# State-space loop of a two-layer backbone: scan states in PSUM, all back rotations on VectorE, the last gelu product on GpSimd, modulation in sixteen pieces

## Chip, core, metric

The kernel runs on one core of a Trainium2 chip. The metric is the device time of one launch in microseconds (us). The engines are TensorE (PE in the profile), VectorE (DVE), ScalarE (ACT), GpSimd (POOL) and SyncE (SP), which issues the DMAs. Each works through its own queue in order and waits for the others by semaphores. Operands lie in SBUF or in PSUM, the eight banks into which TensorE writes.

## What is computed

A backbone of two layers over 1024 latent tokens and 256 context tokens, 1024 wide. Layer 0 mixes with differential attention, layer 1 with a bidirectional diagonal state-space layer (S5). The change lies in that state-space layer:

```python
def step(h, uc):
    bu = jnp.einsum('gpc,btgc->btgp', b_bar, uc.astype(jnp.complex64))
    a_cum, hs = lax.associative_scan(_linear_combine, (a, bu), axis=1)
    hs = hs + a_cum * h[:, None]
    y = jnp.real(jnp.einsum('gcp,btgp->btgc', c_mat, hs))
    return hs[:, -1], y
...
g = jax.nn.gelu(y.astype(h.dtype))
o1, o2 = jnp.split(jnp.einsum('btd,de->bte', g, w_glu), 2, axis=-1)
return o1 * jax.nn.sigmoid(o2)
```

There are 64 channel groups of 16 channels with 64 complex states each, a forward and a backward direction, and `a` is the same at every token. Beside it each layer needs six modulation vectors (shift, scale and gate, twice) from a product of one row with a 1024 x 6144 matrix, `ada_w`.

## The kernel before

The complex recurrence is made real by a rotation: the inputs are turned back by the angle that the state has gained up to their place, a real scan with the decay alone runs over the places, and its states are turned forward again. The method `s5` does it in `for n in range(19)`, which is written in software-pipelined form; for ScalarE, VectorE, GpSimd and TensorE the order of the code is the order of the queues (`with self.manual()`), only SyncE's is set by a scheduler. Step n takes the four channel groups 4n to 4n+3 for n up to 15; d is 0 forward and 1 backward. The parts, with the engine:

- `phase(n, d)` (GpSimd): the angles, an integer add of 128 x 640, into one of three buffers `phs`, which it may overwrite when the back rotations of three directions earlier have read it.
- `trig(n, d)` (ScalarE, four instructions): sine and cosine in place; `decay(n, d)` (ScalarE): the decay of each place into `rs`.
- `inputs(n, d)` (TensorE): the scan inputs into PSUM, two matrices j of 128 x 640 (`xbank`), four matmuls each. The profile shows each of these matmuls as two rows.
- `rotate(n, d)` (VectorE, two products from PSUM into `t1` and `t2`), and the sum `t1 + t2` (GpSimd).
- `scan(n, d)` (VectorE): the recurrence, 128 x 640, decay and input from SBUF.
- `back(n, d, j)` (four products of 128 x 512): states times cosine and sine into `cs`. Three are on VectorE; the last, backward, j = 1, is on GpSimd at the start of the next step.
- `outputs(n)` (TensorE, one step later): for each of four groups i five matmuls into bank 6 or 7.
- gelu of step m = n - 2: Square (ScalarE), `scalar_tensor_tensor` (VectorE), Tanh and `u + 1` (ScalarE), the product with y (VectorE) into `ggs`. The buffer `u` is one for all steps.
- `tr` (TensorE): four transposes into the bank whose output the gelu has read. At odd n they read the product of the same step, at even n older ones. `tr_out` (ScalarE, then VectorE in the next step): their result, split into a high and a low part.
- `modulation(i)`: one of eight halves of the layer's last four modulation vectors, 32 matmuls, a copy on ScalarE, a transpose, and two small VectorE instructions. Its weights (2 MB) are loaded over the part of `U` that the loop has consumed: `mods` holds for each half the step at whose end it is loaded and the step at whose end it is multiplied (20: behind the loop).

Behind the loop follow the last modulation halves, the last products of the GLU's first weight block (`first`), and the GLU itself.

Of the kernel before, what the change touches and what calls it, by code (L numbers as in the profile page):

```python
# [6 lines left out]
F32 = mybir.dt.float32  # L7
# [63 lines left out]
class Prog:  # L71
# [192 lines left out]
    def ada_half_load(self, ws, l, seg, half):  # L264
        c0 = 1024 * seg + 512 * half
        for kk, w in enumerate(ws):
            self.dma(w, self.I["ada_w"][l].rearrange("(k p) n -> p k n", p=128)[:, 2 * kk : 2 * kk + 2, c0 : c0 + 512])

    def ada_half_products(self, ws, l, seg, half, acc, t=None):
        nc = self.nc  # L270
        for k in range(8):
            for j in range(4):
                nc.tensor.matmul(acc[32 * j : 32 * j + 32], self.scT[:, 2 * k : 2 * k + 32],
                                 ws[k // 2][:, k % 2, 128 * j : 128 * j + 128], start=k == 0, stop=k == 7)
# [7 lines left out]
        nc.vector.scalar_tensor_tensor(m, acc.rearrange("p (j r) -> p r j", j=4)[:, 0:2], 1.0 if seg in (1, 4) else 0.0, m,  # L282
                                       ALU.add, ALU.add)
# [1569 lines left out]
    def s5(self):  # L1853
# [7 lines left out]
        u = self.fv(36, 4, 8, 16)  # L1861
# [6 lines left out]
        cs = [[(self.fv(x, 4, 128), self.fv(y, 4, 128)) for x, y in (((10, 32), (29.5, 34)), ((15, 22.5), (17.5, 22.5)))[d]]  # L1868
# [9 lines left out]
        mods = [(6, 8), (8, 10), (10, 12), (11, 13), (12, 14), (13, 15), (15, 20), (15, 20)]  # L1878
        halves = [[self.view(self.U, 16 * i + 4 * kk, (2, 512)) for kk in range(4)] for i in range(2)]
# [11 lines left out]
        def modulation(i, c):  # L1891
            self.ada_half_products(halves[i % 2 if i > 2 else 0], 1, 2 + i // 2, i % 2, self.PS[:, c : c + 128])
# [24 lines left out]
        def xbank(n, d, j):  # L1917
            b = 1024 * ((4 * n + 2 * d + j) % 3)
# [24 lines left out]

        def scan(n, d):
            t1, t2, r = (t.rearrange("p x n -> p (x n)") for t in (*ts[d][n % 2], rs[d][n % 2]))
            v.tensor_tensor_scan(t2, r, t1, 0.0, ALU.mult, ALU.add)

        def back(eng, n, d, j):
# [5 lines left out]
            eng.tensor_tensor(o, ts[d][n % 2][1][:, :, h], (Ps if j else Pc)[:, :, h], ALU.mult)  # L1954

        def outputs(n):
# [622 lines left out]
```

## Time and profile before

| | |
|---|---|
| median of 3 runs | 2849.98 us (2846.97 to 2850.45) |
| profiled execution | span 2849.8 us, 0.2 under the median; no other time of it is shown |
| TensorE, VectorE, ScalarE, GpSimd busy over the whole span | 96%, 71%, 48%, 36% |
| start of the forward scan of step 0, 2 and 15 | 1832.71, 1855.02, 2004.43 us |
| first matmul of `first(1, ...)`, behind the last modulation half | 2030.70 us |

A row of the timeline has the start from the span's beginning, the duration, engine, line and operation, the tiles (`FD` and `U` are SBUF, `PS` is PSUM, `H` and `W` are SBUF) and the number of equal instructions merged in it; a bracket at its end tells how long the engine stood idle before it and what ended that. Neighbouring instructions of one engine overlap by up to 0.1 us, so that what one costs is read from start to start. A row of the stretches has, for each engine, its busy time in the stretch, and at the end the clock granted to TensorE, the share of the DMA engines and the rate in GB/s. A row of the groups has the number of instructions, the busy time and the mean in ns of one, and the idle time before them.

### The profile page before, as it was taken

Reading aid. Unit: us, or ns where it says so; the run is one execution under the profiler, and the core shown is the slowest. Engines: PE = TensorE matmul, PEld = TensorE weight load, DVE = VectorE, ACT = ScalarE, POOL = GpSimd, SP = SyncE. Lnnn points to the kernel's source line nnn. Section 1 sums busy time; section 2 is a strip of 40 time slices with the busy share of each in tenths; the row PEclk is TensorE's granted clock in tenths of the full one; section 3 lists DMA queues with packets and bytes.
Section 4 is the critical chain, followed back from the end, with each engine's and each line's share of the span. In section 5 each row is a group of like instructions: output and inputs, shape, how many; then the busy total and the mean of one; then the engine's idle time right before and its main releaser. Section 6 shows DMA issues by size and latency. Waiting matters only on the chain.

```text
span 2849.8 us, 43385 instructions
## 1 busy us (share of the span) xinstructions
PE 2723.3 (96%) x15229; PEld 2283.1 (80%) x15229; DVE 2019.8 (71%) x2984; ACT 1369.5 (48%) x2583; POOL 1037.2 (36%) x901
## 2 busy tenths in 40 slices
PE   6999999999999999999999999789999999999999
PEld 4688888888877887778877878688887778888887
DVE  6357788888873667767698878799543597668466
ACT  3425555565653753333444445487444633344443
POOL 3314676766663600000030013688121143336414
PEclk9999999999999999999999999899999999999999
DMA  9955555655825359886799878579742144476544
GB/s 279 319 172 188 152 173 172 177 171 171 256 91 182 128 179 316 294 302 216 249 312 310 272 238 263 169 228 306 235 154 98 66 163 160 155 246 227 167 131 142
DMA packets 414823, 586.30 MB, mean 206 GB/s; under 512 B 41870, under 2 KB 260236, under 8 KB 411404
## 3 DMA queue, kind: packets, MB, share of 16 engines
q1 hardware_dynamic: 414604, 583.52, 63.5%
q8 instruction: 120, 1.97, 0.3%
q14 instruction: 99, 0.81, 0.1%
HBM read 396.38 MB, written 182.82 MB: 203 GB/s over the span
## 4 chain that ended last, share of the span: by engine, by line
PE 76%; DVE 9%; DMA 5%; issue 4%; POOL 3%; ACT 2%; SPq 1%; DVEq 0%; ACTq 0%; POOLq 0%
PE PS L132 21%; PE PS L134 20%; PE PS L133 20%; PE PS L581 4%; PE PS L627 2%; PE PS L1928 2%; PE PS L1963 2%; DMA FU<-in_mlp_w 1%; DMA Ta<-FU 1%; PE PS L202 1%; DVE R L138 1%; SPq L80 1%; DVE F L615 1%; ACT F L604 1%; DVE H L138 1%
## 5 line engine op out<-in xcount | busy, mean ns | idle before, releaser
L132 PE MATMUL PS<-H 128*128 128x512 f32 x1072 | 420.6, 393 | 2.7 <-ACT H L137 1.7
L134 PE MATMUL PS<-H 128*128 128x512 f32 x1072 | 417.5, 390 | 2.8 <-DVE H L138 1.5
L133 PE MATMUL PS<-H 128*128 128x512 f32 x1072 | 417.7, 390 | 0.0
L132 PE MATMUL PS<-H,R 128*128 128x512 f32 (+1 forms) x828 | 308.0, 374 | 4.3 <-ACT R L137 2.0
L133 PE MATMUL PS<-H,R 128*128 128x512 f32 (+1 forms) x828 | 298.6, 361 | 0.0
L134 PE MATMUL PS<-H,R 128*128 128x512 f32 (+1 forms) x828 | 298.0, 361 | 0.0
L132 PEld LDWEIGHTS PS<-H 128*128 128x128 f32 x1072 | 201.2, 188 | 50.5 <-issue 6.4
L134 PEld LDWEIGHTS PS<-H 128*128 128x128 f32 x1072 | 201.2, 188 | 46.1 <-DVE H L138 2.3
L133 PEld LDWEIGHTS PS<-H 128*128 128x128 f32 x1072 | 201.3, 188 | 40.6
L604 ACT ACTIVATE F<-F,stat 128x1280 f32<-128x1280 f32 x128 | 174.3, 1362 | 106.6 <-DVE F L594 106.5
L137 ACT ACTIVATE H<-U 128x640 fp32r<-128x640 f32 x216 | 131.9, 674 | 172.6 <-PE PS L133 138.3
L137 ACT ACTIVATE R<-W 128x512 fp32r<-128x512 f32 (+1 forms) x184 | 128.7, 707 | 174.1 <-PE PS L133 101.5
L132 PE MATMUL PS<-R,H 128*128 128x512 f32 x520 | 208.0, 401 | 3.3 <-ACT H L137 3.3
L134 PE MATMUL PS<-R,H 128*128 128x512 f32 x520 | 205.0, 396 | 1.8 <-DVE H L138 1.8
L133 PE MATMUL PS<-R,H 128*128 128x512 f32 x520 | 204.5, 394 | 0.0
L138 DVE TENSOR_TENSOR H<-U,H 128x640 fp32r<-128x640 f32 x216 | 165.1, 797 | 50.6 <-ACT H L137 49.6
L138 DVE TENSOR_TENSOR H<-W,H 128x512 fp32r<-128x512 f32 (+1 forms) x137 | 125.2, 924 | 102.8 <-ACT H L137 102.1
L594 DVE TENSOR_SCALAR_CACHE_REDUCE F<-PS 128x1280 f32<-128x1280 f32 x128 | 185.2, 1483 | 9.3 <-PE PS L581 9.1
L137 ACT ACTIVATE H<-W 128x512 fp32r<-128x512 f32 (+2 forms) x158 | 95.4, 613 | 188.7 <-PE PS L133 116.8
L132 PEld LDWEIGHTS PS<-H,R 128*128 128x128 f32 x828 | 157.6, 191 | 30.2 <-issue 4.1
L134 PEld LDWEIGHTS PS<-H,R 128*128 128x128 f32 x828 | 157.0, 190 | 25.2 <-issue 0.8
L641 POOL TENSOR_SCALAR R<-F 128x256 fp32r<-128x256 f32 (+1 forms) x128 | 126.5, 989 | 136.0 <-ACT F L640 122.4
(534 smaller groups left out, 6860.0 us busy)
## 6 DMA issues: line engine op xcount, KB each, us to landing
W<-in_mlp_w SPq DMA_DIRECT2D x176, 256.0 KB
U<-Aa SPq DMA_DIRECT2D x108, 320.0 KB
Aa<-FU SPq DMA_DIRECT2D x91, 320.0 KB
Ad<-F SPq DMA_DIRECT2D x112, 256.0 KB
W<-Ad SPq DMA_DIRECT2D x112, 256.0 KB
FU<-in_mlp_w SPq DMA_DIRECT2D x32, 512.0 KB
Ta<-FU SPq DMA_DIRECT2D x16, 1024.0 KB
U<-in_ada_w SPq DMA_DIRECT2D x32, 512.0 KB
```

Of the source, the lines that this page charges most:

```text
L132: mm(out, ah, bh, start=first, stop=False, **kw)
L133: mm(out, ah, bl, start=False, stop=False, **kw)
L134: mm(out, al, bh, start=False, stop=last, **kw)
L137: self.nc.scalar.activation(hi, src, AF.Copy)
L138: (lo_eng or self.nc.vector).tensor_tensor(lo, src, hi.bitcast(F32), ALU.subtract)
L581: mm(self.PS[:, 1280 * c + k0 : 1280 * c + k1], Q[:, c, r, qs], K[c][:, k0:k1], start=r == 0, stop=r == 1)
L594: ts(p[c], self.PS[:, 1280 * c : 1280 * c + 1280], 1.0, None, ALU.mult, ALU.min, accum_out=sm[:, c : c + 1])
L604: nc.scalar.activation(p[c], p[c], AF.Exp, bias=sm[:, c : c + 1], scale=-1.0, accum_out=sn[:, 0:1] if c else s0[:, u + 1 : u + 2])
L627: self.nc.tensor.transpose(tb[:, 128 * (kt - k0) : 128 * (kt - k0) + 128], w[:, 128 * kt : 128 * kt + 128], self.ident)
L641: nc.gpsimd.tensor_scalar(hi, t, 1.0, 0.0, ALU.mult, ALU.add)
L1928: mm(b[:, o : o + 160], X[:, d, i, 64 * j : 64 * j + 128], U[:, 4 * n + i, cols], start=True, stop=True)
L1963: mm(o, cs[d][n % 2][j][:, i], W[:, d, i], start=False, stop=d == 1 and j == 1)
```

## The change

Four things are changed in `s5`, with what they need around them.

1. `scan` writes its states to PSUM, columns 2048 to 2687, one buffer for both directions, instead of `t2`. For that `xbank` uses two areas (j = 0 and 1) for every step and direction instead of three in rotation.
2. All four back rotations are on VectorE and read the states from PSUM; the backward j = 1 outputs have two buffers.
3. Up to m = 14, ScalarE copies y to SBUF (`yc`) instead of making u + 1, and GpSimd makes u + 1 and the last product.
4. The modulation halves are cut into pieces: 16 of 1 MB with 16 matmuls each; the copy, the transpose and the small instructions follow a second piece. They start at step 3 and are multiplied one step after their load in most cases. The two small VectorE instructions go through PSUM where there is a gain.

Besides, the low part of `tr_out` stands ahead of the forward rotations, the first of the four output groups stands between the forward and the backward inputs on TensorE, and the backward `decay` moves behind `yc` on ScalarE. `FD` grows from 56 to 60 KB.

```diff
-    def ada_half_products(self, ws, l, seg, half, acc, t=None):
+    def ada_half_products(self, ws, l, seg, half, part, acc):
         nc = self.nc
-        for k in range(8):
+        for k in range(4 * part, 4 * part + 4):
             for j in range(4):
                 nc.tensor.matmul(acc[32 * j : 32 * j + 32], self.scT[:, 2 * k : 2 * k + 32],
-                                 ws[k // 2][:, k % 2, 128 * j : 128 * j + 128], start=k == 0, stop=k == 7)
-        if t is None:
-            t = self.adat[:, 0:128]
-            nc.scalar.activation(t, acc, AF.Copy)
-        else:
-            nc.vector.tensor_copy(t, acc)
+                                 ws[k // 2 % 2][:, k % 2, 128 * j : 128 * j + 128], start=k == 0, stop=k == 7)
+        if part == 0:
+            return
+        t = self.adat[:, 0:128]
+        nc.scalar.activation(t, acc, AF.Copy)
         nc.tensor.transpose(acc, t, self.ident)
         m = self.modc[:, l, seg, :, 4 * half : 4 * half + 4]
-        nc.vector.scalar_tensor_tensor(m, acc.rearrange("p (j r) -> p r j", j=4)[:, 0:2], 1.0 if seg in (1, 4) else 0.0, m,
-                                       ALU.add, ALU.add)
-        if seg in (1, 2, 4, 5):
+        a = acc.rearrange("p (j r) -> p r j", j=4)[:, 0:2]
+        gain = seg in (1, 2, 4, 5)
+        nc.vector.scalar_tensor_tensor(a if gain else m, a, 1.0 if seg in (1, 4) else 0.0, m, ALU.add, ALU.add)
+        if gain:
             g = self.ng[:, l, {1: 0, 2: 1, 4: 2, 5: 3}[seg], 4 * half : 4 * half + 4]
-            nc.vector.tensor_tensor(m, m, bcast(g, 1, 2), ALU.mult)
+            nc.vector.tensor_tensor(m, a, bcast(g, 1, 2), ALU.mult)
...
-        cs = [[(self.fv(x, 4, 128), self.fv(y, 4, 128)) for x, y in (((10, 32), (29.5, 34)), ((15, 22.5), (17.5, 22.5)))[d]]
+        cs = [[(self.fv(x, 4, 128), self.fv(y, 4, 128)) for x, y in (((10, 32), (29.5, 34)), ((15, 22.5), (17.5, 58)))[d]]
...
-        mods = [(6, 8), (8, 10), (10, 12), (11, 13), (12, 14), (13, 15), (15, 20), (15, 20)]
-        halves = [[self.view(self.U, 16 * i + 4 * kk, (2, 512)) for kk in range(4)] for i in range(2)]
+        mods = [(3, 4, 0), (4, 5, 0), (5, 6, 0), (6, 7, 1), (7, 8, 0), (8, 9, 1), (9, 10, 0), (10, 11, 1), (11, 12, 0), (12, 13, 1),
+                (13, 14, 0), (13, 14, 2), (14, 15, 1), (15, 16, 2), (15, 20, 0), (15, 20, 1)]
+        pieces = [[self.view(self.U, 8 * i + 4 * kk, (2, 512)) for kk in range(2)] for i in range(3)]
...
-            b = 1024 * ((4 * n + 2 * d + j) % 3)
+            b = 1024 * j
...
+        states = shaped(self.PS[:, 2048:2688], (4, 160))
+
         def scan(n, d):
-            t1, t2, r = (t.rearrange("p x n -> p (x n)") for t in (*ts[d][n % 2], rs[d][n % 2]))
-            v.tensor_tensor_scan(t2, r, t1, 0.0, ALU.mult, ALU.add)
-
-        def back(eng, n, d, j):
+            o, r, t1 = (t.rearrange("p x n -> p (x n)") for t in (states, rs[d][n % 2], ts[d][n % 2][0]))
+            v.tensor_tensor_scan(o, r, t1, 0.0, ALU.mult, ALU.add)
+
+        def back(n, d, j):
             Ps, Pc = phs[(2 * n + d) % 3]
             o = cs[d][n % 2][j]
             if d:
                 o = bass.AP(o.tensor, o.offset + 127, [list(o.ap[0]), [128, 4], [-1, 128]])
             h = slice(31, 159)
-            eng.tensor_tensor(o, ts[d][n % 2][1][:, :, h], (Ps if j else Pc)[:, :, h], ALU.mult)
-
-        def outputs(n):
+            v.tensor_tensor(o, states[:, :, h], (Ps if j else Pc)[:, :, h], ALU.mult)
+
+        def outputs(n, groups):
             X, W1, T, W2, _ = slots[n % 2]
-            for i in range(4):
+            for i in groups:
...
-                if 1 <= n <= 16:
-                    back(pool, n - 1, 1, 1)
                 if gelu:
                     act.activation(u, y, AF.Square, scale=float(np.sqrt(0.044715)))
                 if n == 17:
@@ -2012,25 +2013,30 @@
                 if run:
                     if n:
                         trig(n, 1)
-                        decay(n, 1)
                     inputs(n, 0)
                 if 0 < n < 15:
                     phase(n + 1, 0)
+                if lo and n != 17:
+                    lo()
                 if run:
                     rotate(n, 0)
-                if lo and n != 17:
-                    lo()
                 if gelu:
                     v.scalar_tensor_tensor(u, u, 1.0, y, ALU.add, ALU.mult)
                     if n == 17:
                         lo()
                     act.activation(u, u, AF.Tanh, scale=float(np.sqrt(2.0 / np.pi)))
+                if 1 <= n <= 16:
+                    outputs(n - 1, (0,))
                 if run:
                     inputs(n, 1)
                     t1, t2 = ts[0][n % 2]
                     pool.tensor_tensor(t1, t1, t2, ALU.add)
-                if gelu:
+                if gelu and m < 15:
+                    act.activation(yc, y, AF.Copy)
+                elif gelu:
                     act.activation(u, u, AF.Copy, bias=1.0)
+                if 0 < n < 16:
+                    decay(n, 1)
                 if 0 < n < 15:
                     trig(n + 1, 0)
                     decay(n + 1, 0)
@@ -2041,14 +2047,20 @@
                     scan(n, 0)
                 if gelu:
                     gv = ggs[m // 2 % 2].rearrange("p t g c -> p g t c")
-                    v.tensor_tensor(gv[:, 4 * (m % 2) : 4 * (m % 2) + 4], u, y, ALU.mult)
+                    gv = gv[:, 4 * (m % 2) : 4 * (m % 2) + 4]
+                    if m < 15:
+                        pool.tensor_scalar(u, u, 1.0, 1.0, ALU.add, ALU.mult)
+                        pool.tensor_tensor(gv, u, yc, ALU.mult)
+                    else:
+                        v.tensor_tensor(gv, u, y, ALU.mult)
                 if run:
-                    back(v, n, 0, 0)
-                    back(v, n, 0, 1)
+                    back(n, 0, 0)
+                    back(n, 0, 1)
                     scan(n, 1)
-                    back(v, n, 1, 0)
+                    back(n, 1, 0)
+                    back(n, 1, 1)
                 if 1 <= n <= 16:
-                    outputs(n - 1)
+                    outputs(n - 1, (1, 2, 3))
...
-            modulation(6, 1856)
-            modulation(7, 1600)
+            modulation(14)
+            modulation(15)
```

GpSimd's queue over one step in the middle of the loop, before. The rows are the forward sum, the backward sum, the backward `phase` of step n + 1, the last `back` of step n and the forward `phase` of step n + 2; names like `DVE_49` are the semaphores of the engines waited for.

```order
L2031 TENSOR_TENSOR FD<-FD 128x640 [waits DVE_49]
L2040 TENSOR_TENSOR FD<-FD 128x640 [waits DVE_49]
L1908 TENSOR_TENSOR FD<-FD 128x640 [waits DVE_49,Activation_49]
L1954 TENSOR_TENSOR FD<-FD 128x4x128 [waits DVE_49,PE_49,Activation_49]
L1908 TENSOR_TENSOR FD<-FD 128x640 [waits Pool_49]
```

The same of the change: u + 1 (L2052) and the product (L2053) stand behind the backward sum.

```order
L2033 TENSOR_TENSOR FD<-FD 128x640 [waits DVE_49]
L2046 TENSOR_TENSOR FD<-FD 128x640 [waits DVE_49]
L2052 TENSOR_SCALAR FD<-FD 128x512 [waits Activation_49]
L2053 TENSOR_TENSOR FD<-FD 128x4x8x16 [waits Activation_49,Pool_49]
L1909 TENSOR_TENSOR FD<-FD 128x640 [waits DVE_49] x2
```

What moved: both `phase` adds now stand together behind the product, and the back rotation is gone from this queue.

TensorE's queue from the transposes at the end of an odd step to the inputs and outputs of the next, before (L1967 transposes, L1928 inputs, L1960 and L1963 outputs):

```order
L1967 MATMUL PS<-ident,FD 128x128 [waits DVE_49]
L1967 MATMUL PS<-ident,FD 128x128 x3
L1928 MATMUL PS<-U,H 128x160 [waits DMAHW6_49]
L1928 MATMUL PS<-U,H 128x160 x11
L1928 MATMUL PS<-U,H 128x160 [waits DVE_49]
L1928 MATMUL PS<-U,H 128x160 x3
```

And of the change (L1970 transposes, L1929 inputs, L1963 and L1966 outputs):

```order
L1970 MATMUL PS<-ident,FD 128x128 [waits Pool_49]
L1970 MATMUL PS<-ident,FD 128x128 x3
L1929 MATMUL PS<-U,H 128x160 [waits DMAHW6_49]
L1929 MATMUL PS<-U,H 128x160 x7
L1963 MATMUL PS<-W,U 128x128 [waits DMAHW7_49,DVE_49]
L1966 MATMUL PS<-W,FD 128x128 [waits DMAHW1_49]
L1966 MATMUL PS<-W,FD 128x128 [waits DMAHW3_49,DMAHW2_49]
L1966 MATMUL PS<-W,FD 128x128 x2
L1929 MATMUL PS<-U,H 128x160 [waits DVE_49]
L1929 MATMUL PS<-U,H 128x160 x3
L1929 MATMUL PS<-U,H 128x160 [waits DVE_49]
L1929 MATMUL PS<-U,H 128x160 x3
```

What moved: the transposes of an odd step wait for GpSimd instead of VectorE, one output group stands among the inputs, and both halves of the backward inputs wait for rotations instead of the last one alone.

More of the change, by code (lines that the diff above doesn't have):

```diff
@@ L1860, in s5 @@
         ggs = [self.view(self.U, 48, (8, 8, 16)), self.fv(38, 8, 8, 16)]
-        u = self.fv(36, 4, 8, 16)
+        u, yc = self.fv(36, 4, 8, 16), self.fv(56, 4, 8, 16)
         r8 = self.r8
@@ L1889, in first, with modulation @@
                          k == 0, False)
-        def modulation(i, c):
-            self.ada_half_products(halves[i % 2 if i > 2 else 0], 1, 2 + i // 2, i % 2, self.PS[:, c : c + 128])
+        def modulation(i):
+            self.ada_half_products(pieces[mods[i][2]], 1, 2 + i // 4, i // 2 % 2, i % 2, self.PS[:, 2880:3008])
         def load_x(n):
@@ L2058, in s5 @@
                     tr(6, 0, bank)
-                for i, (a, b) in enumerate(mods):
+                for i, (a, b, _) in enumerate(mods):
                     if n == b:
-                        modulation(i, 1856)
+                        modulation(i)
                 if n == 17:
@@ L2068, in s5 @@
                     tr((n - 3) // 2, 1 - n % 2, bank)
-                for i, (a, b) in enumerate(mods):
+                for i, (a, b, j) in enumerate(mods):
                     if n == a:
-                        self.ada_half_load(halves[i % 2 if i > 2 else 0], 1, 2 + i // 2, i % 2)
+                        self.ada_half_load(pieces[j], 1, 2 + i // 4, i // 2 % 2, i % 2)
                 if n + 2 < 16:
@@ L2522, in run @@
             with pool("u") as up, pool("fd") as fp:
[L2523 removed]
+                self.U, self.F = up.tile([128, 62 * KB], F32, name="U"), fp.tile([128, 60 * KB], F32, name="FD")
                 self.mlp0_down()
```

5 lines of the change are left out of this document (2 added, 3 removed).

## Prediction

> **What bounds it now.** I read the page's head first, then the busy times by stretch, then the timelines of the four engines over one step of the state-space loop, then the groups for GpSimd's prices.
>
> ```profile
> span 2849.8 us, 43385 instructions
> PE 76%; DVE 9%; DMA 5%; issue 4%; POOL 3%; ACT 2%; SPq 1%; DVEq 0%; ACTq 0%; POOLq 0%
> ```
>
> TensorE carries the end of the whole program; VectorE is 9% of it. The change lies in one stage, so the stage is what counts. Its stretches, marked off by the starts of forward scans (step 2 at 1855.02, step 15 at 2004.43; 13 steps of the loop between) and by TensorE's first matmul behind the stage (2030.70):
>
> ```profile
> core 0: us, PE busy (x) PEld busy (x) DVE busy (x) ACT busy (x) POOL busy (x), PEclk, DMA share, GB/s
> 1855.02:2004.43 149.41, 135.43 (x1308) 129.17 (x1308) 146.70 (x163) 117.75 (x188) 122.50 (x64) 1.00 0.89 272
> 1866.07:1921.35 55.28, 48.56 (x381) 46.27 (x380) 55.10 (x60) 44.66 (x71) 47.60 (x25) 1.00 0.75 229
> 1924.00:2012.00 88.00, 80.65 (x928) 76.32 (x926) 85.86 (x99) 64.20 (x104) 67.12 (x36) 1.00 1.01 314
> ```
>
> In five undisturbed steps (second row, 11.06 us each) VectorE is busy 55.10 of 55.28: it is the bound there. TensorE has 48.56, GpSimd 47.60: both close behind. Thirteen bare steps would be 143.7; the other 5.7 of the 149.41 is what the modulation halves add. One step, from forward scan to forward scan, VectorE and then GpSimd:
>
> ```profile
> 1899.24 1.49 DVE L1946 TENSOR_TENSOR_SCAN FD<-U,FD 128x640 f32<-128x640 f32 x1
> 1900.64 0.66 DVE L2044 TENSOR_TENSOR U<-FD,PS 128x512 f32<-128x512 f32 x1
> 1901.22 2.00 DVE L1954 TENSOR_TENSOR FD<-FD 128x512 f32<-128x512 f32 x2
> 1903.14 1.48 DVE L1946 TENSOR_TENSOR_SCAN FD<-U,FD 128x640 f32<-128x640 f32 x1
> 1904.66 1.58 DVE L1954 TENSOR_TENSOR FD<-FD 128x512 f32<-128x512 f32 x1
> 1906.16 1.54 DVE L1937 TENSOR_TENSOR FD<-PS,FD 128x640 f32<-128x640 f32 x2
> 1907.63 0.68 DVE L1972 SCALAR_TENSOR_TENSOR H<-PS,H 128x512 fp32r<-128x512 f32 x1
> 1908.23 0.67 DVE L2024 SCALAR_TENSOR_TENSOR FD<-FD,PS 128x512 f32<-128x512 f32 x1
> 1908.82 1.54 DVE L1937 TENSOR_TENSOR FD<-PS,FD 128x640 f32<-128x640 f32 x2
> 1910.29 1.49 DVE L1946 TENSOR_TENSOR_SCAN FD<-U,FD 128x640 f32<-128x640 f32 x1
> ...
> 1897.65 1.56 POOL L2031 TENSOR_TENSOR FD<-FD 128x640 f32<-128x640 f32 x1
> 1899.39 2.67 POOL L2040 TENSOR_TENSOR FD<-FD 128x640 f32<-128x640 f32 x1 [0.19 <-DVE FD L1937]
> 1903.37 2.33 POOL L1908 TENSOR_TENSOR FD<-FD 128x640 int32<-128x640 int32 x1 [1.30 <-ACT H L1971]
> 1905.65 1.73 POOL L1954 TENSOR_TENSOR FD<-FD 128x512 f32<-128x512 f32 x1
> 1907.46 1.28 POOL L1908 TENSOR_TENSOR FD<-FD 128x640 int32<-128x640 int32 x1
> ```
>
> The two engines block each other. The same sum takes GpSimd 1.56 beside rotations (L1937) and 2.67 beside a scan (L1946); the same phase add 1.28 and 2.33. In each slow case GpSimd finishes as if it had begun 1.28 after the scan's start (1905.70 less 1.28 is 1904.42; the scan started 1903.14). A back rotation (L1954) stands in its turn: it needs 1.50 to the next start at 1904.66, where the gelu product, as long but with one operand in PSUM, needs 0.58. What takes part in the blocking has two SBUF inputs; rotations and the gelu product, with one, do not.
>
> **VectorE's side of the change.** Four back rotations now read the states in PSUM: I price each as the gelu product, 0.58 (nearest row, same size, one PSUM operand); three cost 3.42 today (1901.22 to 1903.14 and 1904.66 to 1906.16). The gelu product leaves (0.58). The first back rotation waits for its scan's end, 1.51 instead of 1.40. The step on VectorE becomes scans 3.0, backs 4 x 0.58 plus 0.1 for the wait at the second scan, two rotation pairs 2.93, low part 0.60, gelu's first product 0.59: 9.6 against 11.05. That would be 13 x 1.45 = 19 us, if VectorE stayed the bound. I find that it does not.
>
> **GpSimd's new chain.** GpSimd loses one back rotation and gets a tensor_scalar (u+1) and the product, ahead of the backward phase add of the next step. Prices, without a scan beside them, for two inputs at 512 elements and one input at 1024; then the sine/cosine chain on ScalarE:
>
> ```profile
> L1343 POOL TENSOR_TENSOR FA<-FA,FB 128x512 f32<-128x512 f32 x4 | 5.2, 1298 | 0.3
> L356 POOL TENSOR_SCALAR F<-F,stat 128x1024 f32<-128x1024 f32 x8 | 9.5, 1189 | 0.4
> ...
> 1905.73 0.74 ACT L1912 ACTIVATE FD<-FD 128x640 f32<-128x640 int32 x1 [1.96 <-POOL FD L1908]
> 1907.89 0.74 ACT L1915 ACTIVATE FD<-FD 128x640 f32<-128x640 f32 x1
> ```
>
> The product is 1.30. The tensor_scalar lies between half of 1.19 (0.60) and the product's 1.30; I take 0.67, near the half, as it has one input. From the forward scan's start (0) of a step: the backward sum ends at 2.82, as now (1902.06). Then tensor_scalar to 3.49. The backward scan, which waited for the sum, takes the shared access at about 3.4 and GpSimd gets in 1.28 later, at 4.68. (If the scan gets it first, tensor_scalar and product follow it and the end is within 0.2.) Product to 5.98, phase add to 7.26, the four ScalarE steps from 1905.73 to 1908.63, 2.90, to 10.19 with the hand-over of 0.03, the backward rotations 1.47 to 11.71, and the next forward scan starts. Each link waits for the one before in its own queue, so a step lasts **11.71, not 9.6**: today the phase add ends at 6.46 and nothing stands behind it but VectorE. Behind GpSimd's queue also wait the forward phase add and the forward sum of the next step; they end before 10.2 and cost nothing. ScalarE's Square waits for the product too (u has one buffer), at 6.0 to 6.6, covered by the phase add.
>
> **TensorE in odd steps.** At the end of an odd step the four transposes need this step's product, and they stand ahead of the next step's inputs on TensorE:
>
> ```profile
> 1901.88 0.60 PE L1967 MATMUL PS<-ident,FD 128*128 128x128 f32 x4
> 1902.32 3.43 PE L1928 MATMUL PS<-U,W 128*128 128x160 f32 x24
> 1907.03 1.35 PE L1928 MATMUL PS<-U,W 128*128 128x160 f32 x8 [1.29 <-DVE FD L1937]
> ...
> 1986.45 4.51 PE L1928 MATMUL PS<-U,H 128*128 128x160 f32 x32
> 1990.80 0.39 PE L1960 MATMUL PS<-W,U 128*128 128x128 f32 x2
> 1991.91 0.39 PE L1960 MATMUL PS<-W,U 128*128 128x128 f32 x2
> ```
>
> Product 5.98, hand-over 0.06, transposes 0.44, all 32 input rows (two rows a matmul) 4.35 and the one output group that now stands among them 1.11: 11.94; the last eight drain in 0.26 (1.35 against 1.09), hand-over 0.05, second rotation 0.73: **12.98**. Today the product comes at 1901.30, before TensorE asks for it. That inputs now reuse two bank pairs instead of three puts rotations one after another behind TensorE, up to 0.5 a step; in both walks it is inside. The modulation pieces (half a half each, about 1 us of TensorE) fall where TensorE waits for the product, so I cost them at nothing; that cover goes if the product comes early.
>
> Sum over the 13 steps: 7 behind even numbers x 11.71 and 6 behind odd ones x 12.98 = 159.9 against 149.41: **+10.4**.
>
> **The ends.** Step 0 loses its third bank pair while TensorE is slow: eight rows take 2.50 there against 1.35, and the last rotation of three packed ones waits for them. Between 0 and 2.5; I take 1.
>
> ```profile
> 1830.26 2.25 DVE L1937 TENSOR_TENSOR FD<-PS,FD 128x640 f32<-128x640 f32 x3
> 1840.65 2.50 PE L1928 MATMUL PS<-U,W 128*128 128x160 f32 x8 [6.03 <-DVE FD L1937]
> ...
> 2025.28 1.95 PE L273 MATMUL PS<-U,scT 128*32 128x128 f32 x64
> 2028.22 1.96 PE L273 MATMUL PS<-U,scT 128*32 128x128 f32 x64 [0.26 <-DVE modc L282]
> 2030.70 0.48 PE L132 MATMUL PS<-H 128*128 128x512 f32 x1
> ```
>
> Behind the loop, two halves (5.42) become two pieces, one half in all (2.94): -2.5. A piece in step 16 goes back on TensorE's path, about 1.9, and the half of step 15 leaves it, about 1: -1.6 in all, between -4 and 0. Together 10.4 + 1 - 1.6 = +9.8, on a span of 2849.8, which agrees with the median of 2849.98 within 0.2: **2860 us**, 0.35% slower. A measurement here tells 0.2% (5.7 us) from no change.
>
> **A rule on the blocking.** The rows show the blocking only for scans that write SBUF; the new ones write PSUM. The Trainium skill, "SBUF — State Buffer", section "Who interferes with whom", says that a VectorE instruction with two SBUF inputs contends with a GpSimd instruction that reads SBUF, and one with at most one does not, whichever starts first blocking the other whole. The rows above agree (2.67 against 1.56). By that rule the new scans block as before and the sum stays 2860; if the output's place decided instead, it would be the first rival's 2839.
>
> **Rivals.** *Faster: scans into PSUM leave GpSimd free.* The sum would end at 0.15 + 1.56, tensor_scalar, product and phase add at 4.96, sines at 7.9: under VectorE's 9.6. TensorE then bounds: 4.35 + 4 x 1.11 + 0.44 = 9.2, a piece 1.0, in every second step copy and transpose 0.9: 10.7. 13 x 10.7 = 139 instead of 149.4, with the ends -11: 2839. It decides once the two waits, 1.1 and 1.2 a step, fall by 0.8 together. For it: no row has such a scan. Against: rotations write SBUF and do not block, so inputs, not outputs, tell them apart. *Same: TensorE does not stand in odd steps*, because the product is ready sooner than I price or another link is shorter; then 13 x 11.71 = 152.2, +2.8, with the ends +2.2: 2852. *Slower still: late pieces.* A piece now has one step to land instead of two. Record (2.1 MB by the shapes in the code) and piece (1.05 MB) per step at the 314 GB/s of the saturated stretch take 10.0 of 12.3 us, so it should fit; late by 1 us in 12 steps gives 2872.
>
> **Chances.** Forecast 0.50, first rival 0.18, second 0.17, third 0.07; 0.05 for a smaller gain and 0.03 for no change in other ways. Slower 0.57, same 0.20, faster 0.23. The forecast's own range is 2854 to 2867 (tensor_scalar 0.60 to 1.30, the ends' bounds); to leave out two in ten it must reach the first rival: 2838 to 2869.
>
> **What would show it.** Right: forward scans 11.7 and 13.0 apart in turn; the backward phase add ending about 7.3 behind the forward scan's start; the transposes of odd steps waiting for GpSimd; VectorE's rotations waiting for ScalarE and TensorE; its busy share under 0.85; back rotations near 0.66. Wrong: sums beside a scan at 1.56, or scans evenly under 11 apart.

## The result: 2.3% slower, over six times the loss foreseen

The changed kernel takes 2916.6 us (median of 4 runs, 2911.55 to 2921.41) against 2850.22 for the kernel before beside it (4 runs, 2846.97 to 2855.07): a ratio of 1.0231 [1.0217, 1.0244]. The forecast was 2860. The sign was right and the size was not: +66 us instead of +10.

The first view is that of the stretches, of the kernel after: the 13 loop steps from the forward scan of step 2 to that of step 15, then four single steps (2, 3, 8 and 9).

```profile
core 0: us, PE busy (x) PEld busy (x) DVE busy (x) ACT busy (x) POOL busy (x), PEclk, DMA share, GB/s
1861.35:2074.30 212.95, 165.20 (x1376) 156.77 (x1375) 135.55 (x166) 117.71 (x189) 123.18 (x77) 0.82 0.66 206
1861.35:1872.84 11.49, 10.81 (x85) 10.27 (x84) 9.41 (x12) 8.41 (x14) 9.55 (x6) 1.00 0.75 247
1872.84:1888.14 15.30, 10.60 (x67) 10.41 (x66) 10.37 (x13) 9.89 (x17) 9.57 (x6) 0.78 0.50 158
1953.91:1970.72 16.81, 13.17 (x111) 12.50 (x110) 10.38 (x14) 8.89 (x15) 9.57 (x6) 0.80 0.70 219
1970.72:1988.00 17.28, 13.25 (x112) 12.51 (x111) 10.54 (x14) 9.17 (x16) 9.58 (x6) 0.80 0.61 199
```

The loop grew from 149.41 to 212.95. The two profiled executions differ by 69.8 us: +63.5 in the loop, -2.7 behind it in the stage, +6.3 ahead of the first scan, a place that varies from execution to execution, and +2.6 behind the stage. Step 2, even and without a piece, lasts 11.49. Step 3, odd and still without a piece, lasts 15.30. With pieces both kinds last about 17 from step 6 on (16.81 and 17.28 in steps 8 and 9). In steps 3, 8 and 9 no engine is near full (the busiest, TensorE, has 13.17 of 16.81), and the clock granted to TensorE, 1.00 over the loop before, is 0.82 over this loop: the engines wait for each other, and TensorE runs slowly for part of the time.

Who waits, over the whole program (engine, its tile and line, what it waited for; total us, times, longest):

```profile
PE PS L273 <- DVE FD L1957: 40.0, 11, 3.6
PE PS L1970 <- POOL U L2053: 8.1, 2, 4.7
```

The first row is the new one: the modulation pieces (L273) stand 3.6 us, eleven times, for VectorE's back rotations (L1957). Their operands have nothing to do with each other. The pieces accumulate in columns 2880 to 3007 of PSUM, the states lie in 2048 to 2687; but a bank has 512 columns (`bank(i)` in the kernel), so bank 5 (2560 to 3071) holds the end of the states and the accumulator. The waits in the program go by banks, which e7 below shows with one number. The Trainium skill, "PSUM — Partial Sum Buffer", section "PSUM bank collisions raise a hardware error", says the same as a rule: two engines are kept apart by bank, not by address. The row above agrees.

TensorE's timeline, first in step 3, then in step 9 with a piece (rows in between are left out here and below):

```profile
1878.71 1.11 PE L1970 MATMUL PS<-ident,U 128*128 128x128 f32 x4 [4.70 <-POOL U L2053]
1879.62 4.39 PE L1929 MATMUL PS<-U,H 128*128 128x160 f32 x16
1884.96 2.34 PE L1929 MATMUL PS<-U,H 128*128 128x160 f32 x16
...
1976.85 1.93 PE L273 MATMUL PS<-U,scT 128*32 128x128 f32 x32 [3.64 <-DVE FD L1957]
1979.45 1.06 PE L1970 MATMUL PS<-ident,FD 128*128 128x128 f32 x4
1980.31 3.56 PE L1929 MATMUL PS<-U,H 128*128 128x160 f32 x16
```

Sixteen input rows (L1929) take 2.34 us at 1884.96 and 4.39 at 1879.62, the same instruction behind an idle time of 4.70. The transposes need 1.11 instead of 0.60. That is the clock at half: the granted clock is 0.53 from 1880 to 1884 and 1.00 from 1884 to 1886. And behind the piece everything queues that the next step needs: transposes, inputs, and with them the rotations.

GpSimd and VectorE in step 2, where the forecast's chain can be read without the pieces:

```profile
1861.35 1.49 DVE L1949 TENSOR_TENSOR_SCAN PS<-U,FD 128x640 f32<-128x640 f32 x1
1862.88 1.29 DVE L1957 TENSOR_TENSOR FD<-PS,FD 128x512 f32<-128x512 f32 x2
1864.29 1.82 DVE L1949 TENSOR_TENSOR_SCAN PS<-U,FD 128x640 f32<-128x640 f32 x1
1871.37 1.55 DVE L1938 TENSOR_TENSOR FD<-PS,FD 128x640 f32<-128x640 f32 x2 [1.88 <-ACT FD L1916]
...
1861.51 2.66 POOL L2046 TENSOR_TENSOR FD<-FD 128x640 f32<-128x640 f32 x1 [1.24 <-ACT U L1943]
1864.15 0.61 POOL L2052 TENSOR_SCALAR FD<-FD 128x512 f32<-128x512 f32 x1
1864.85 2.33 POOL L2053 TENSOR_TENSOR U<-FD 128x512 f32<-128x512 f32 x1
1867.13 2.51 POOL L1909 TENSOR_TENSOR FD<-FD 128x640 int32<-128x640 int32 x2
```

A scan that writes PSUM blocks GpSimd as one that writes SBUF did: the sum beside it takes 2.66. The product waits once more for the backward scan (2.33), and the backward rotations (1871.37) wait for the sines behind the phase add.

### The profile page after: what moved, and what is told of

It is laid out like the page before. It is cut to its first block, busy times and chain, and to the rows that moved or that the text cites. A ratio compares the mean times of both kernels' runs of the same rounds, so it can differ in the third digit from the quotient of the medians.

```text
span 2919.6 us, 43387 instructions
## 1 busy us (share of the span) xinstructions
PE 2756.3 (94%) x15229; PEld 2311.1 (79%) x15229; DVE 2001.3 (69%) x2985; ACT 1367.7 (47%) x2583; POOL 1034.3 (35%) x915
## 4 chain that ended last, share of the span: by engine, by line
PE 73%; DVE 11%; DMA 7%; ACT 3%; POOL 3%; issue 3%; SPq 1%; DVEq 0%; ACTq 0%; POOLq 0%
PE PS L132 20%; PE PS L134 20%; PE PS L133 19%; PE PS L581 4%; PE PS L1929 3%; PE PS L627 2%; DMA FU<-in_mlp_w 2%; DVE PS L1949 1%; DMA Ta<-FU 1%; DVE R L138 1%; DVE FD L1957 1%; DMA W<-in_mlp_w 1%; PE PS L273 1%; PE PS L202 1%; DVE H L138 1%
## 5 line engine op out<-in xcount | busy, mean ns | idle before, releaser
L132 PEld LDWEIGHTS PS<-H,R 128*128 128x128 f32 x828 | 157.5, 190 | 31.3 <-issue 4.1
L134 PEld LDWEIGHTS PS<-H,R 128*128 128x128 f32 x828 | 157.5, 190 | 25.4 <-issue 0.8
```

Source lines behind the costliest of these rows:

```text
L132: mm(out, ah, bh, start=first, stop=False, **kw)
L134: mm(out, al, bh, start=False, stop=last, **kw)
```

## Experiments

Four causes were to be told apart. A: the shared bank. B: GpSimd's chain with the product. C: TensorE's clock after idle times. D: other edits of the change. The parts of the program ahead of and behind the stage vary from execution to execution (the first forward scan starts between 1826.95 and 1839.05), so beside the ratio of whole runs the table gives two times of the profiled execution. Each ratio is to runs of before taken beside that kernel, and their median lies between 2850.22 and 2853.0, so the medians in the table can't be divided by its first row. "Loop" is scan of step 2 to scan of step 15; "stage" is scan of step 0 to the first matmul of `first(1, ...)`.

| kernel | median us | ratio to before | loop | stage |
|---|---|---|---|---|
| before | 2850.22 | | 149.41 | 197.99 |
| after | 2916.6 | 1.0231 [1.0217, 1.0244] | 212.95 | 258.83 |
| e1_halves | 2877.6 | 1.0091 [1.0064, 1.0119] | 171.06 | 222.56 |
| e2_gelu_on_vector | 2917.97 | 1.0233 [1.0210, 1.0256] | 212.78 | 259.34 |
| e3_both | 2852.2 | 1.0001 [0.9986, 1.0016] | 148.64 | 194.74 |
| e4_warm | 2893.9 | 1.0151 [1.0119, 1.0183] | 191.49 | 240.32 |
| e5_halves_warm | 2868.93 | 1.0061 [1.0046, 1.0077] | 161.53 | 216.56 |
| e6_unsplit | 2850.0 | 1.0001 [0.9992, 1.0010] | 147.65 | 195.32 |
| e7_halves_bank5 | 2883.43 | 1.0119 [1.0105, 1.0133] | 178.50 | 229.66 |
| e8_transposes_later | 2875.99 | 1.0091 [1.0078, 1.0105] | 161.35 | 216.26 |
| e9_low_part_after | 2845.34 | 0.9974 [0.9961, 0.9988] | 143.71 | 191.13 |
| e10_pieces_in_gap | 2854.56 | 1.0002 [0.9991, 1.0014] | 146.98 | 196.92 |

### e1_halves: the change without the pieces

```diff
-        mods = [(3, 4, 0), (4, 5, 0), (5, 6, 0), (6, 7, 1), (7, 8, 0), (8, 9, 1), (9, 10, 0), (10, 11, 1), (11, 12, 0), (12, 13, 1),
-                (13, 14, 0), (13, 14, 2), (14, 15, 1), (15, 16, 2), (15, 20, 0), (15, 20, 1)]
+        mods = [(6, 8), (8, 10), (10, 12), (11, 13), (12, 14), (13, 15), (15, 20), (15, 20)]
...
-            self.ada_half_products(pieces[mods[i][2]], 1, 2 + i // 4, i // 2 % 2, i % 2, self.PS[:, 2880:3008])
+            self.ada_half_products(halves[i % 2 if i > 2 else 0], 1, 2 + i // 2, i % 2, self.PS[:, c : c + 128])
```

Here c is 1856 inside the loop, and a half is multiplied, copied and transposed at once.

> The changed kernel with the modulation of before: whole halves of 32 matmuls, their accumulator in bank 3 (column 1856) at the steps of before; everything else of the change stays. Theory A (the pieces share PSUM bank 5 with the states, so on TensorE they and all behind them wait for the last back rotation): the wait of L273 for L1957 goes, even steps stay near 11.5, odd ones fall from 15.3 to 17.3 to about 13 to 14, 13 loop steps take about 165, the kernel about 2866 us (2858 to 2878). Rival B (the GpSimd chain with the gelu product alone makes the steps long, the pieces only lie beside it): steps stay at 15 to 17, the kernel stays over 2900.

The loop falls by 41.9 and the kernel by about 39. That is A's direction. But the odd steps 3 to 9 stay at 15.5 to 15.8 (1867.46 to 1883.08 below) where A gave 13 to 14, and TensorE shows why, without any piece:

```profile
1873.32 1.11 PE L1969 MATMUL PS<-ident,U 128*128 128x128 f32 x4 [4.70 <-POOL U L2052]
1874.23 4.47 PE L1928 MATMUL PS<-U,H 128*128 128x160 f32 x16
```

```profile
1867.46:1883.08 15.62, 10.92 (x67) 10.73 (x66) 10.38 (x14) 10.12 (x17) 9.57 (x6) 0.78 0.51 155
1883.08:1894.57 11.49, 9.86 (x82) 9.62 (x81) 10.01 (x13) 7.77 (x13) 9.54 (x6) 1.00 0.73 230
```

The columns are those of the stretches above. In the odd step the granted clock is 0.78, in the even one 1.00. The odd steps 11 and 13 of the same run, where the clock stayed up (1.00 in both), last 12.83 and 12.86. The accumulator's new place, bank 3, isn't free either: the second input area ends there, at column 1855. But the rotations have long read it when a half comes, and no idle time ahead of a half in the loop ends with a VectorE rotation.

### e2_gelu_on_vector: the change without GpSimd's product

```diff
-                    if m < 15:
-                        pool.tensor_scalar(u, u, 1.0, 1.0, ALU.add, ALU.mult)
-                        pool.tensor_tensor(gv, u, yc, ALU.mult)
+                    v.tensor_tensor(gv, u, y, ALU.mult)
```

(and `u + 1` on ScalarE in place of `yc`, as before.)

> The changed kernel with u + 1 on ScalarE and the last gelu product on VectorE, as before; the pieces in bank 5 stay. Theory A: TensorE still stands until the last back rotation, about 6.0 us behind the forward scan's start, then piece 1.1 to 2.3, transposes, 32 input rows and one output group, last rotation 6.9: 14 to 15.5 a step, the kernel 2885 to 2905 us. Rival B (GpSimd chain alone): steps of about 10.5, the kernel about 2840.

Rival B is out: with the pieces in place, the move of the product costs nothing at all (212.78 against 212.95). The wait is the same and comes once more:

```profile
PE PS L273 <- DVE FD L1957: 44.9, 12, 3.8
```

A missed on the size: it had expected 14 to 15.5 a step and 2885 to 2905 us, and from step 4 on it is 16.8 to 18.1 a step, with 0.80 of the clock in step 4, and 2918 us.

### e3_both: neither

Both edits together.

> Halves of before and the gelu product on VectorE: what is left of the change is the states in PSUM, four back rotations on VectorE, two input areas and the new order. Theory A with the GpSimd chain as the second cause: VectorE about 10.2 a step, TensorE 9.2 and the halves, 13 steps about 140, the kernel 2838 to 2846 us, faster than before. If scans into PSUM or the two input areas cost by themselves: 2855 or more.

The loss is gone: 1.0001. But the gain isn't there. GpSimd's product, which costs nothing beside the pieces, costs 22.4 us of loop without them (171.06 against 148.64): the two losses lie beside each other, and the longer one shows. What holds e3 at 11.28 a step is seen on TensorE and VectorE:

```profile
1902.55 0.49 PE L1962 MATMUL PS<-H,U 128*128 128x128 f32 x2 [1.76 <-DVE H L1974]
1903.77 2.34 PE L1928 MATMUL PS<-U,W 128*128 128x160 f32 x16
...
1905.13 0.82 DVE L1937 TENSOR_TENSOR FD<-PS,FD 128x640 f32<-128x640 f32 x1 [0.57 <-PE PS L1928]
1906.21 0.83 DVE L1937 TENSOR_TENSOR FD<-PS,FD 128x640 f32<-128x640 f32 x1 [0.26 <-PE PS L1928]
```

The output group that the change puts between the inputs writes the bank that the low part (L1974) still reads. TensorE waits 1.76 for that, and VectorE 0.83 for the inputs behind it.

### e4_warm: the change with TensorE kept busy

```diff
+                if 4 <= n < 16:
+                    for _ in range(8):
+                        mm(self.PS[:, 832:960], self.ident, self.ident, start=True, stop=True)
                 for i, (a, b, _) in enumerate(mods):
                     if n == b:
                         modulation(i)
```

> The changed kernel with eight matmuls of the identity by itself into unused columns of bank 1, on TensorE in steps 4 to 15 behind the output groups, ahead of the piece: about 3 us of work inside a wait of 3.6 to 4.7 us. Theory C (TensorE's clock falls to about half after that idle, and the slow matmuls behind it are a large part of the loss): the 16 input rows take 2.3 again instead of 4.4, steps shorten by 1.5 to 2.5, the kernel 2885 to 2900 us. If the clock is no part: same time, 2912 to 2920, or slower by what the matmuls take.

As C expected: 96 matmuls more, and the kernel is about 23 us faster. The order of the work is that of the change, and only the idle time ahead of the pieces is shorter:

```profile
1944.96 1.95 PE L2073 MATMUL PS<-ident 128*128 128x128 f32 x16
1948.76 1.08 PE L273 MATMUL PS<-U,scT 128*32 128x128 f32 x32 [1.85 <-DVE FD L1957]
1949.78 0.66 PE L1970 MATMUL PS<-ident,U 128*128 128x128 f32 x4
1950.27 2.34 PE L1929 MATMUL PS<-U,W 128*128 128x160 f32 x16
```

The piece takes 1.08 instead of 1.93, the input rows 2.34 instead of 3.5 to 3.8. Even steps fall from about 16.8 to 14.1, odd ones from about 17.3 to between 14.7 and 16.4. Of the 63.5 us that the loop lost, this takes back 21.5, and that is a lower bound for the clock: step 3, which got no such matmuls, stays at 15.43, and three of the odd steps still have a clock of 0.90 (see the last section).

### e5_halves_warm: the case that the prediction summed

e1 with matmuls of the identity ahead of the transposes of odd steps:

```diff
+                if n % 2 and 3 <= n < 15:
+                    for _ in range(12):
+                        mm(self.PS[:, 832:960], self.ident, self.ident, start=True, stop=True)
                 if 3 <= n < 19 and n != 15:
                     tr((n - 3) // 2, 1 - n % 2, bank)
```

> e1_halves with twelve matmuls of the identity by itself ahead of the transposes of odd steps (3 to 13), about 2.9 us inside the wait for GpSimd's product of 3.4 to 4.7 us. In e1_halves the odd steps last 15.5 to 15.8, with 16 input rows at 4.47 instead of 2.34. Theory C (what the blind sum missed in odd steps is TensorE's clock after a long idle): odd steps fall to the 13.0 that the sum gave, even ones stay at 11.5, six times 2.6 less: about 2862 us. If the matmuls only fill the wait: 2877 as e1_halves.

This takes away the two things that the prediction had not seen, the bank and the clock, and leaves those that it had summed. Odd steps without a half last 12.83 to 12.85 (summed: 12.98), even ones 11.49 (11.71):

```profile
1865.18:1878.01 12.83, 10.81 (x91) 10.62 (x90) 10.29 (x13) 9.64 (x17) 9.57 (x6) 1.00 0.57 187
1878.01:1889.50 11.49, 9.87 (x82) 9.63 (x81) 10.01 (x13) 8.15 (x13) 9.55 (x6) 1.00 0.77 233
1853.69:2015.22 161.53, 150.05 (x1455) 145.41 (x1454) 134.86 (x164) 116.73 (x188) 123.30 (x77) 1.00 0.84 257
```

The loop, 161.53, stands against 159.9 in the sum, but that closeness is partly luck. Bare steps at the measured 11.49 and 12.84 would make 157.5; the halves, which the sum put at nothing, add 2.4, and the added matmuls cost 1.7 in step 13, where a half already fills the wait (14.54 against 12.86 in e1). The kernel is at 2869 and not 2862: the stage is 18.6 longer than before, 12.1 of it in the loop; in the last steps, which got no such matmuls, one more idle time of 3.37 us halves the clock.

### e6_unsplit and e9_low_part_after: the rest of the order undone

```diff
-                if 1 <= n <= 16:
-                    outputs(n - 1, (0,))
...
-                    outputs(n - 1, (1, 2, 3))
+                    outputs(n - 1, (0, 1, 2, 3))
```

> e3_both with all four output groups behind the backward inputs again, as before. In e3_both VectorE stands 0.83 us a step for inputs that stand behind an output group, which waits 1.76 us for the low part (L1974). Theory D (that edit of the change costs what the cheaper back rotations bring): steps fall from 11.28 to about 10.2, 13 steps about 136 instead of 148.6, the kernel about 12 us below e3_both, 2838 to 2842, faster than before. If something else sets the 11.28: same as e3_both.

A miss: bare steps are 10.89, not 10.2, and the kernel is as fast as before, not faster. The wait of 1.76 is gone. What is left are the two waits of VectorE for inputs, 0.19 and 0.26 a step: with two input areas instead of three, the backward inputs stand until the forward rotations have read theirs. So e9 puts these rotations ahead of the low part again:

```diff
-                if lo and n != 17:
-                    lo()
                 if run:
                     rotate(n, 0)
+                if lo and n != 17:
+                    lo()
```

> e6_unsplit with the low part (L1974) behind the forward rotations again, as before, instead of ahead of them. In e6_unsplit VectorE stands 0.19 and 0.26 us a step for inputs whose areas the forward rotations free; 0.60 us earlier rotations would cover both: steps of 10.4 to 10.5 instead of 10.89, steps with a half stay near 12.1, the kernel 3 to 6 us below e6_unsplit (2844 to 2848), which 5 rounds may only just tell from before. If the waits move elsewhere: same as e6_unsplit, 2850.

```profile
1877.88:1919.45 41.57, 38.07 (x306) 37.10 (x305) 40.70 (x53) 36.63 (x57) 32.07 (x16) 1.00 0.80 241
1857.10:2000.81 143.71, 134.00 (x1313) 129.42 (x1312) 133.15 (x178) 118.65 (x187) 102.98 (x51) 1.00 0.93 276
```

Four bare steps take 41.57, 10.39 each, VectorE 98% busy in them: it is the bound again, at a lower level than the 11.06 of before. The kernel is a little faster than before, 0.9974 [0.9961, 0.9988], some 7 us, and the stage of its profiled execution is 6.9 shorter. It keeps of the change the states in PSUM, the two input areas, the four back rotations on VectorE and the later `decay`; the product, the halves and the order on TensorE and VectorE are those of before. The steps with a half, 12.0 to 12.2, gained nothing.

### e7_halves_bank5: one number

```diff
-                        modulation(i, 1856)
+                        modulation(i, 2880)
```

> e3_both with one number changed: the accumulator of the halves inside the loop at column 2880, in bank 5 with the states, instead of 1856 in bank 3. Theory A (sharing a bank with the states makes a product wait for the last back rotation): the steps with a half (six of them) grow from 11.86 to about 15 to 17, the kernel 20 to 32 us above e3_both, 2872 to 2884. Rival: it was the cutting into pieces or their shorter time to land; then no difference to e3_both.

This is e3 with the accumulator of its halves moved to the states' bank. Nothing else differs, and it costs 30 us of loop, 28 of them in the five steps of the loop with a half, which grow from 11.86 to between 17.1 and 18.1. The waits, then the row of one:

```profile
PE PS L273 <- DVE FD L1956: 22.2, 6, 3.8
```

```profile
1925.55 3.64 PE L273 MATMUL PS<-U,scT 128*32 128x128 f32 x64 [3.77 <-DVE FD L1956]
```

So cause A is shown by itself: it needs neither the cutting into pieces nor a late load. And the half takes 3.64 instead of 1.96: behind this wait the clock is at half too.

### e8_transposes_later: the product off TensorE's path

e1 with the transposes of odd steps behind the forward inputs of the next step:

```diff
+                if n % 2 == 0 and 4 <= n <= 14:
+                    inputs(n, 0)
+                    tr((n - 4) // 2, 0, other)
                 lo = tr_out((n - 4) // 2, n % 2, other) if n >= 4 and n != 17 else None
```

> e1_halves with the transposes of odd steps (3 to 13) behind the forward inputs of the next step on TensorE, so that these no longer queue behind GpSimd's product. If the transposes carry the product's lateness into the step: odd steps fall from 15.6 to the 11.5 to 12 of even ones, the kernel about 2853 (2849 to 2860). If the lateness comes by another way (Square waiting for the product, the phase add): odd steps stay above 14 and the kernel above 2868.

The odd steps in the middle fall from 15.7 to 12.35, so the lateness did come through the transposes, most of it by the clock: e5, which left them in place, had brought the same steps to 12.85. TensorE waits 1.55 there instead of 3.7, at full clock:

```profile
1922.49 2.34 PE L1928 MATMUL PS<-U,H 128*128 128x160 f32 x16
1926.38 0.66 PE L1969 MATMUL PS<-ident,U 128*128 128x128 f32 x4 [1.55 <-POOL U L2056]
1928.44 0.49 PE L1962 MATMUL PS<-W,U 128*128 128x128 f32 x2 [1.41 <-DVE H L1974]
```

Three odd steps stay at 13.5 to 14.0: steps 3 and 11, with a clock of 0.88, and step 13, with a half. The forecast (2849 to 2860 us) was a miss: the loop is 9.7 shorter than in e1, but the kernel is not, 1.0091 both. Against before, the profiled execution is 25.0 longer: 18.3 in the stage, 4.3 ahead of it and 2.4 behind it. Whether the part outside belongs to the edit stays open.

### e10_pieces_in_gap: the pieces in the same bank, at another place

e9 with sixteen pieces in bank 5, multiplied between the forward and the backward inputs, where TensorE waits anyway and no states are alive (from step 5 on, one a step in most, two in steps 12 and 15; one half, two pieces, is left behind the loop):

```diff
+                here = [i for i, (a, b, _) in enumerate(mods) if n == b]
+                whole = [i for i in here if i % 2]
+                for i in here:
+                    modulation(i)
+                if whole:
+                    self.ada_half_copy(macc)
...
+                if whole:
+                    columns(whole[0])
                 if run:
                     scan(n, 0)
```

> e9 with the sixteen pieces of the change, still accumulated in bank 5, but multiplied between the forward and the backward inputs on TensorE, in a wait of 1.38 us, when the last back rotation has read the states and the next scan has not begun; copy ahead of Tanh, columns ahead of the forward scan. Theory A (not the pieces, only their place against the states in that bank was wrong): no wait for L1956, no idle over 1.5 us, full clock, even steps with a piece 10.5 to 11.2, 13 steps 138 to 145, one half less behind the loop: 2836 to 2846 us, faster than before. Rival (pieces as such, by their shorter time to land or their bank, cost 3 us or more a step): over 2870.

```profile
1910.15 1.08 PE L273 MATMUL PS<-U,scT 128*32 128x128 f32 x32 [1.31 <-DVE FD L1964]
1911.16 2.44 PE L1936 MATMUL PS<-U,H 128*128 128x160 f32 x16
...
2004.34 1.93 PE L273 MATMUL PS<-U,scT 128*32 128x128 f32 x32 [3.49 <-DVE FD L1964]
```

At the new place a piece waits 1.31 for the back rotation in some steps and not at all in the others, where the inputs behind it waited 1.38 for rotations in e6, and the clock over the loop is 1.00. Against e2, which has the pieces at their old place and the product on VectorE too, the loop is 66 us shorter, with the same bank; two edits of the order are undone as well, which were worth 4.9 between e3 and e9. The rival is out at the price that it named, 3 us or more a step. One part of it this run doesn't touch: most pieces are loaded two steps ahead here, one step in the change. But in the change, too, no idle time ahead of a piece ends with a DMA, and e7 has the wait with halves loaded as before. The forecast was too good, though (2836 to 2846 us): steps with one piece last 10.6 to 11.9 and the two with two pieces 13.0, so e9's halves are cheaper. And in step 16, which has no inputs for the piece to stand between, the old trap is back (last row: 3.49 of waiting, 1.93 for the piece). Equal to before, 1.0002.

## Why the prediction was wrong, step by step

**The step that failed: "The modulation pieces ... fall where TensorE waits for the product, so I cost them at nothing".** The cover named was the wait for the product, and the pieces' own start was not asked for. But a piece does not start in that wait; it waits itself, for the last back rotation, by the bank that it shares with the states (3.6 us, eleven times; e7 shows it by one number). It stands ahead of the transposes and inputs, so it passes its wait on, in even steps too, where the sum had no wait of TensorE at all. Against the same kernel with halves in bank 3 this costs 41.9 us of loop (e1 against after). The listing of TensorE's queue ahead of the prediction begins at the transposes, behind L273, so this wait is not on it.

**The step that was not there: the clock.** The sum priced TensorE's rows at their price of before, where the quoted loop steps have no wait over 1.29 us and a clock of 1.00. The forecast itself made TensorE stand 3 to 4 us in odd steps, and did not ask what that does to the rows behind it: 16 rows at 4.4 instead of 2.34. The prediction's own rows of step 0 had the sign, eight input rows at 2.50 instead of 1.35 behind an idle time of 6.03, and it used them for step 0 alone. Filling the waits took back 21.5 us in the change (e4) and 9.5 with halves (e5 against e1; 11.2 in the four slow odd steps, less the 1.7 that the filling cost).

**The odd step, 12.98,** measured 15.30 (step 3, no piece). With the clock held it is 12.83 to 12.85 (e5): the links were right and the price of one of them wrong.

**GpSimd's chain, 11.71,** measured 11.49 (step 2, and the even steps of e1 and e5). Its terms as listed end at 11.66; the other 0.05 has no name. The blocking by scans into PSUM was right (2.66 beside a scan, forecast as 2.67), tensor_scalar took 0.61 (forecast 0.67), the product 2.33 with its wait. The Trainium skill's rule in "SBUF — State Buffer", section "Who interferes with whom", that two SBUF inputs make a VectorE instruction contend, holds for these scans; where the output goes did not matter.

**VectorE's prices.** A back rotation from PSUM measures 0.60 from start to start (two in 1.2), forecast 0.58. Its terms add up to 9.54, not 9.6. The sum could only be read in e9, with the gelu product back on VectorE: 10.39 against 9.6 + 0.58 = 10.2.

**The ends.** Step 0 to step 2 takes 22.30 against 22.31 before (forecast +1, measured 0; 22.0 to 23.1 in the experiments, which have the same two areas). Behind the last forward scan TensorE reaches `first(1, ...)` after 23.58 instead of 26.27: -2.7, forecast -1.6.

**The rivals.** "Scans into PSUM leave GpSimd free" is refuted by 2.66. "Late pieces" had the right culprit and the wrong mechanism, with +1 us a step where it was +4 to +5: no idle time ahead of a piece ends with a DMA, and the DMA share in such steps is 0.6 to 0.75. "TensorE does not stand in odd steps" is refuted by the 4.70.

With the terms that the runs give, the loop adds up by the order in which they were taken away: 149.41 before; to 161.53 with the chain and the transposes (e5, +12.1, summed as +10.4); to 171.06 with the clock in odd steps (e1, +9.5); to 212.95 with the pieces in bank 5 (+41.9, clock included). The chain and the transposes alone already make the kernel slower (e5, 1.0061), so the sign was not luck; the size was missed by the other two. The terms are no independent prices: e2 shows that GpSimd's chain is worth nothing once the pieces wait.

## What to carry to other kernels

Before an accumulator is put into "free" PSUM columns, ask by banks who else is there at that moment, and what stands behind the new instruction on TensorE; in the same bank, at a place where the states were dead, the pieces made the loop 66 us shorter (e10 against e2, the order undone as well). A forecast that leaves TensorE idle for 3.4 us or more, as here, has to reckon with half the clock for what follows, and shorter waits are no guarantee of the full one (last section). And when two losses lie side by side, undo both: undoing GpSimd's product alone showed nothing, undoing it without the pieces showed 22 us.

## The hardware: when the clock falls

Four transposes take 0.60 to 0.66 at full clock and 1.11 at half. The rows of these loops show that the length of an idle time alone does not decide between the two. First of e1:

```profile
1955.55 1.11 PE L1969 MATMUL PS<-ident,FD 128*128 128x128 f32 x4 [3.36 <-POOL FD L2052]
1983.18 0.66 PE L1969 MATMUL PS<-ident,U 128*128 128x128 f32 x4 [3.37 <-POOL U L2052]
```

of e8 (its step 3, transposes and the next group):

```profile
1877.09 0.66 PE L1969 MATMUL PS<-ident,U 128*128 128x128 f32 x4 [2.53 <-POOL U L2056]
1879.16 0.80 PE L1962 MATMUL PS<-W,U 128*128 128x128 f32 x2 [1.41 <-DVE H L1974]
```

of e4 (its step 9, a piece and the transposes behind it):

```profile
1962.88 1.08 PE L273 MATMUL PS<-U,scT 128*32 128x128 f32 x32 [1.85 <-DVE FD L1957]
1964.52 1.02 PE L1970 MATMUL PS<-ident,FD 128*128 128x128 f32 x4
```

and of e2 (its step 3, an output group and the inputs behind it):

```profile
1871.52 0.49 PE L1963 MATMUL PS<-W,U 128*128 128x128 f32 x2 [1.86 <-DVE H L1975]
1872.74 4.01 PE L1929 MATMUL PS<-U,H 128*128 128x160 f32 x16
```

After 3.36 the clock was half in one step and full in another of the same kernel; after 3.64 it was nearly always half, for some 3 to 5 us (one piece of the change, in step 5, still ran at full clock). Right behind a wait of 1.85 the pieces of e4 always ran at full clock, but in three odd steps the transposes behind them took 0.81 to 1.06, with one more wait of 0.40 in between. In e8's step 3, 2.53 alone left it full, and a second wait of 1.41 shortly behind brought the slow rows (0.80 for two where 0.49 is usual). And in e2's step 3 a single wait of 1.86 was enough: the two rows behind it are fast, the 16 input rows that follow take 4.01 instead of 2.34, while the same wait of 1.86 in e3's step 3, for the same low part, left them at 2.34. In seven steps of e3 TensorE waits for that low part, 12.3 in all, and its clock over the loop is 1.00.

The Trainium skill, "TensorE: Matmul & The Clock Gate", Part 1, describes a gate at half rate by default that watches free-running windows of about 3.4 us. That equal waits, of 3.36 and of 1.86, fall on either side agrees with a free-running window. What else decides it, these runs do not show.
